# The last down product and the final norm in runs of three, two and one token tiles instead of two runs of three

## The chip, the core and the metric

One NeuronCore of one Trainium2 chip runs the whole program. The metric is the device time of one execution in microseconds (us). The kernel before takes 2925.16 us, the median of three runs (2922.57 to 2926.08).

## What is computed

A two-layer encoder over 256 prompt tokens and 1024 sample tokens, 1024 channels, all in 32-bit floats. Layer 0 mixes with grouped-query attention, layer 1 with a Conformer convolution module; each is followed by a SwiGLU feed-forward network (FFN) of width 2816, and the trunk ends in an RMS norm:

```python
for i in range(DEPTH):
    x = x + mixer(_rms_norm(x, ...))
    x = x + _swiglu(_rms_norm(x, ffn_norm_g[i]), w_gate[i], w_up[i], w_down[i])
return _rms_norm(x, final_norm_g)
```

Here `_swiglu(h) = (silu(h @ w_gate) * (h @ w_up)) @ w_down`, and the norm divides each token's 1024 channels by the root of their mean square and multiplies by `final_norm_g`.

## The kernel before, in words

Activations lie transposed in SBUF: eight tiles `xs[ct]` of 128 channels by tokens. To keep the precision of 32-bit floats each matrix product is made of three matmuls: the left and the right operand are split into a high and a low part (`hl`, `hh`), and high by high, high by low and low by high are added up in PSUM. The tokens go through the layers in two halves; in layer 1 these are CA (tokens 0 to 623) and CB (tokens 624 to 1279, 656 of them). The program's last call is `close(1, rest, xb, CB)`, behind the FFN of CB.

By then all FFN blocks of CB but the last pair of 128 have been multiplied with `w_down` and added to `xs`. `rest` holds that pair. `close` does three things. It multiplies the pair with its rows of `w_down` (`pd`, L1194 to L1197: per channel tile `ct` six matmuls, 2 blocks by 3 parts, of as many columns as the run has tokens). It adds the result to `xs[ct]` (L1200, on VectorE). And it ends with the final norm, for one tile of about 110 tokens at a time: `turn` (L1160) brings the tile to rows of tokens by eight transposes on TensorE into the PSUM tile `fo` (L1164), squares it on ScalarE in two pieces of 512 channels with a sum along the row (L1167, sums in `ssh`), and hands the rest to `finish`, a generator. `finish` adds the two sums (L1172), computes the inverse root on VectorE by a shift and three Newton steps (`rsqrt_steps` and `newton`, L109 to L130: thirteen more operations on one column each), multiplies `fo` by it and by the gain in two pieces (`yo`, L1177), and stores each piece with a DMA from the SyncE queue (L1178).

The tokens are taken in two runs of 328, and each run is three tiles (108, 110, 110). While run 2's channel tiles are multiplied, the tiles of run 1 are turned, one behind each odd `ct`, and `advance(8)` (L1181) takes eight steps of the running generators behind every add from `ct` 3 on, in turns. Behind the last add, `advance(1000)` ends what is still running; then the three tiles of run 2 are turned and finished, with nothing left to multiply.

Two things set the order. `close` stands in a block with `manual_schedule(engines=PE_DVE)` (L1295): TensorE and VectorE execute exactly in the order in which the code issues, so an instruction that waits holds up all behind it on its engine. ScalarE and the queues take what a scheduler gives them. And PSUM is one pool, `pp`, of four buffers of two banks (L640); both `pd` and `fo` come from it (`acc`). A `pd` buffer is free again when its add has read it; a `fo` buffer only when both of its `yo` have.

Of the kernel before, what the change touches and what calls it, by code (L numbers as in the profile page):

```python
# [71 lines left out]
def trunk(ctx: ExitStack, tc: tile.TileContext, a: dict):  # L72
# [33 lines left out]
    def rsqrt_steps(v, shape, scale, eps):  # L106
        rows = shape[0]
        w = small.tile([P, 8], F32, name="rs_w")[:rows, :shape[1]]
        V.tensor_scalar(out=w, in0=v, scalar1=scale, scalar2=eps, op0=ALU.mult, op1=ALU.add)  # L109
        r = small.tile([P, 8], F32, name="rs_r", bufs=5)[:rows, :shape[1]]  # L110
        yield r
        for _ in newton(w, r, *(small.tile([P, 8], dt, name=f"rs_{n}")[:rows, :shape[1]]
                                for n, dt in (("i", I32), ("y", I32), ("t", F32)))):
            yield r
        return r
# [26 lines left out]
    def weights(src, g=None, room=None):  # L142

        raw = wp.tile([P, D], F32, tag="raw", bufs=RAW, name="raw")
        nk = src.shape[1]
        nc.sync.dma_start(raw.rearrange("p (k c) -> p k c", k=nk), src)
        pool, tag, bufs = room or (wp, "hl", WEIGHTS)
        hl = pool.tile([P, 2, D], F32R, tag=tag, bufs=bufs, name="hl")
        if g is None:
            split(hl[:, 0, :], hl[:, 1, :], raw)  # L150
        for k in range(nk if g is not None else 0):
            c = slice(k * D // nk, (k + 1) * D // nk)
            split_scaled(hl[:, 0, c], hl[:, 1, c], raw[:, c], g[:, k:k + 1])
        return hl
# [197 lines left out]
    tiles = [(u, n) for u in us for n in range(len(u.tiles))]  # L352
# [57 lines left out]
    with tc.tile_pool(name="qa", bufs=1) as qa, tc.tile_pool(name="qm", bufs=4, space=PSUM) as qm, \  # L410
# [124 lines left out]
        half = NT // 2  # L535
# [59 lines left out]
        for n, (b, cg) in enumerate(seq):  # L595
            for i in range(half):
                t = b * half + i
# [45 lines left out]
    def slot(name, dt=F32):  # L643
        return sp.tile([P, SLOT], dt, tag="s", name=name)
# [4 lines left out]
    def acc(name):  # L649
        return pp.tile([P, 2, 512], F32, tag="acc", name=name)  # L650
# [502 lines left out]
    def close(layer, rest, xs, half):  # L1153


        n = half.n
        cs = (slice(0, 512), slice(512, D))
        wd = [weights(a["w_down"][layer, f * P:(f + 1) * P, :].unsqueeze(1)) for f, _ in rest]

        def turn(lo, hi):  # L1160
            w = hi - lo
            ps = acc("fo").rearrange("p c n -> p (c n)")[:w]
            for ct in range(NK):
                PE.transpose(ps[:, ct * P:(ct + 1) * P], xs[ct][:, lo:hi], ident)  # L1164
            ss = small.tile([P, 8], F32, name="ssh")
            for k, cc in enumerate(cs):
                S.activation(out=slot("sq")[:w, :512], in_=ps[:, cc], func=AF.Square, accum_out=ss[:w, k:k + 1])  # L1167
            return finish(ps, ss, lo, hi)

        def finish(ps, ss, lo, hi):  # L1170
            w = hi - lo
            V.tensor_tensor(out=ss[:w, 0:1], in0=ss[:w, 0:1], in1=ss[:w, 1:2], op=ALU.add)  # L1172
            yield
            r = yield from rsqrt_steps(ss[:w, 0:1], (w, 1), 1.0 / D, RMS_EPS)
            for cc in cs:
                y = slot("yo")[:w, :512]
                V.scalar_tensor_tensor(out=y, in0=ps[:, cc], scalar=r, in1=gf[:w, cc], op0=ALU.mult, op1=ALU.mult)  # L1177
                nc.sync.dma_start(a["y_sample"][0, half.lo + lo - SP:half.lo + hi - SP, cc], y)  # L1178
                yield

        def advance(steps):  # L1181
            while running and steps:
                g = running.pop(0)
                if next(g, running) is not running:
                    running.append(g)
                steps -= 1

        running, tiles = [], []
        for c in range(2):
            t = slice(c * n, (c + 1) * n)  # L1190
            for ct in range(NK):
                o = slice(ct * P, (ct + 1) * P)
                pd = acc("pd")[:, 0, :n]
                for k, (_, (h, l)) in enumerate(rest):  # L1194
                    for p, x in ((0, h), (0, l), (1, h)):
                        PE.matmul(pd, wd[k][:, p, o], x[:, t], start=k == 0 and p == 0 and x is h,
                                  stop=k == len(rest) - 1 and p == 1)  # L1197
                if ct % 2 == 1 and tiles:
                    running.append(turn(*tiles.pop(0)))
                V.tensor_tensor(out=xs[ct][:, t], in0=pd, in1=xs[ct][:, t], op=ALU.add)  # L1200
                if ct > 2:
                    advance(8)
            cuts = [c * n + n * k // 3 // 2 * 2 for k in range(3)] + [(c + 1) * n]
            tiles = list(zip(cuts, cuts[1:]))
        advance(1000)
        for lo, hi in tiles:
            running.append(turn(lo, hi))
            advance(3)
        advance(1000)
# [85 lines left out]
    with tc.manual_schedule(engines=PE_DVE):  # L1295
        close(1, rest, xb, CB)
# [39 lines left out]
```

## Time and profile before

| | before |
|---|---|
| time, median of 3 runs | 2925.16 us |
| the profiled execution's own time | 2926.48 us |
| its span, first to last instruction | 2924.7 us |
| mean granted TensorE clock | 0.990 |
| TensorE busy | 2837.6 us, 97% |
| VectorE busy | 2291.9 us, 78% |
| ScalarE busy | 1171.2 us, 40% |

The profile shows one execution; its own time is 1.8 us above its span. Busy shares are averages over the whole program. `close` begins at 2887 us from the start of the span and is its last 38 us, so the stretch from there to the end is what has to be read. A granted clock of 1.00 is 2.4 GHz and 0.50 is 1.2 GHz.

### The profile page before, as it was taken

The page shows a single profiled execution, that of the slowest core. Times are in us where ns is not written, and L with a number is a line of the kernel's source. Part 1 is how long each engine was busy: PE and PEld are TensorE (multiplying, and loading weights), DVE is VectorE, ACT ScalarE, POOL GpSimd, SP SyncE. Part 2 cuts the span into 40 slices and gives each one's busy share as a digit, 9 for nine tenths or more (in the row PEclk, how much of TensorE's full clock was granted, in tenths as well). Part 3 has the DMA queues.
Part 4 walks back from the last instruction along what each step waited for, and adds up shares of the span by engine and source line. Part 5 has one row for each costly group of instructions (what it writes and reads, how often), then busy time and mean ns, then how long its engine had stood idle before and what let it go on. Part 6 is the DMA issues. An engine that isn't in the chain of part 4 may idle for free.

```text
span 2924.7 us, 46991 instructions
## 1 busy us (share of the span) xinstructions
PE 2837.6 (97%) x18573; PEld 2717.8 (93%) x18573; DVE 2291.9 (78%) x3741; ACT 1171.2 (40%) x1853; POOL 404.4 (14%) x417
## 2 busy tenths in 40 slices
PE   8998999999999999999999999999999998999997
PEld 6877788789999999999999999999999998999997
DVE  7988999976777777797998666989984538777776
ACT  4538888863433334322111243222223324333332
POOL 2444555420000000010000101110001000000000
PEclk9999999999999999999999999999999999999999
DMA  4513232136777788457676764332324423432221
GB/s 145 189 69 112 51 92 58 45 109 204 257 265 271 274 279 270 126 181 259 217 248 220 277 190 129 115 115 88 99 87 153 128 77 95 134 87 74 86 73 52
DMA packets 316324, 438.68 MB, mean 150 GB/s; under 512 B 22296, under 2 KB 244512, under 8 KB 299208
## 3 DMA queue, kind: packets, MB, share of 16 engines
q1 hardware_dynamic: 298488, 400.10, 42.8%
q0 software_dynamic: 5280, 21.42, 2.0%
q10 hardware_dynamic: 12336, 14.16, 1.4%
q8 instruction: 146, 2.39, 0.3%
q14 instruction: 74, 0.61, 0.1%
HBM read 299.46 MB, written 130.93 MB: 147 GB/s over the span
## 4 chain that ended last, share of the span: by engine, by line
PE 85%; DVE 8%; DMA 3%; issue 2%; ACT 1%; POOL 0%; SPq 0%; DVEq 0%; ACTq 0%; POOLq 0%
PE pd L664 18%; PE ci L1014 8%; PE pg L664 4%; PE pu L664 4%; PE pt L322 4%; PE s L270 4%; PE co L664 4%; PE wo L664 3%; PE z L795 3%; PE z L797 3%; PE z L796 3%; PE v L795 3%; PE v L796 3%; PE v L797 3%; PE y L796 2%; PE y L797 2%
## 5 line engine op out<-in xcount | busy, mean ns | idle before, releaser
L135 ACT CAST hl<-raw 128x1024 fp32r<-128x1024 f32 x328 | 341.2, 1050 | 702.0 <-issue 342.9
L664 PE MATMUL pd<-hh,hl 128*128 128x320 f32 (+2 forms) x2752 | 523.0, 309 | 1.0 <-DVE x L922 0.7
L136 DVE TENSOR_TENSOR hl<-raw,hl 128x1024 fp32r<-128x1024 f32 x328 | 408.3, 1246 | 125.4 <-ACT hl L135 120.0
L1055 DVE SCALAR_TENSOR_TENSOR c<-u,cols,c 128x640 f32<-128x640 f32 (+1 forms) x480 | 429.2, 897 | 8.0
L664 PEld LDWEIGHTS pd<-hh,hl 128*128 128x128 f32 x2752 | 433.4, 188 | 1.8 <-DVE x L922 1.4
L922 DVE TENSOR_TENSOR x<-pd,x 128x640 f32<-128x640 f32 (+2 forms) x304 | 248.6, 823 | 114.8 <-PE pd L664 113.1
L664 PE MATMUL pd<-hl 128*128 128x320 f32 (+2 forms) x1376 | 313.2, 309 | 0.0
L664 PEld LDWEIGHTS pd<-hl 128*128 128x128 f32 x1376 | 230.3, 188 | 0.0
L136 DVE TENSOR_TENSOR pl<-pt,ph 128x512 fp32r<-128x512 f32 x272 | 186.9, 688 | 15.3 <-ACT ph L135 10.8
L282 DVE TENSOR_SCALAR_CACHE_REDUCE s<-s,r_q 128x1024 f32<-128x1024 f32 (+1 forms) x160 | 181.0, 1132 | 20.2 <-PE s L270 13.1
L1014 PE MATMUL ci<-hnh,hl 128*128 128x320 f32 (+2 forms) x1024 | 192.5, 309 | 0.0
L322 PEld LDWEIGHTS pt<-ident,p 128*128 128x128 f32 x1088 | 133.2, 142 | 59.6 <-DVE pl L136 17.2
L315 POOL TENSOR_SCALAR p<-p,rl 128x1024 f32<-128x1024 f32 (+1 forms) x160 | 158.3, 993 | 169.9 <-DVE rl L312 127.1
L135 ACT CAST ph<-pt 128x512 fp32r<-128x512 f32 x272 | 159.7, 589 | 53.7 <-PE pt L322 44.7
L322 PE MATMUL pt<-ident,p 128*128 128x128 f32 x1088 | 167.5, 276 | 13.7 <-DVE pl L136 10.5
L689 POOL TENSOR_TENSOR sq<-sq 128x640 f32<-128x640 f32 (+2 forms) x27 | 51.5, 1906 | 898.9 <-ACT sq L684 555.9
L795 PE MATMUL z<-bh,hl 128*128 128x320 f32 (+1 forms) x528 | 166.1, 315 | 7.9 <-DMA hl<-w_w_up 4.9
L797 PE MATMUL z<-bh,hl 128*128 128x320 f32 (+1 forms) x528 | 165.6, 314 | 2.3 <-DVE hl L136 2.3
L304 ACT ACTIVATE p<-s,nm 128x1024 f32<-128x1024 f32 (+1 forms) x160 | 159.3, 998 | 18.6 <-DVE s L282 18.4
L796 PE MATMUL z<-bl,hl 128*128 128x320 f32 (+1 forms) x528 | 165.5, 313 | 0.0
L1014 PEld LDWEIGHTS ci<-hnh,hl 128*128 128x128 f32 x1024 | 163.9, 188 | 0.0
L664 PE MATMUL pu<-hnh,hl 128*128 128x312 f32 x704 | 132.9, 306 | 0.0
(246 smaller groups left out, 6816.1 us busy)
## 6 DMA issues: line engine op xcount, KB each, us to landing
raw<-in_w_down_dram SPq DMA_DIRECT2D x88, 512.0 KB
raw<-in_w_gate_dram SPq DMA_DIRECT2D x66, 512.0 KB
raw<-in_w_up_dram SPq DMA_DIRECT2D x66, 512.0 KB
w_w_gate<-hl SPq DMA_DIRECT2D x33, 1024.0 KB
w_w_up<-hl SPq DMA_DIRECT2D x33, 1024.0 KB
hl<-w_w_gate SPq DMA_DIRECT2D x33, 1024.0 KB
hl<-w_w_up SPq DMA_DIRECT2D x33, 1024.0 KB
raw<-in_conv_w_in_dram SPq DMA_DIRECT2D x32, 512.0 KB
```

Source lines behind the costliest of these rows:

```text
L135: S.copy(out=dst_h, in_=src)
L136: V.tensor_tensor(out=dst_l, in0=src, in1=dst_h.bitcast(F32), op=ALU.subtract)
L282: V.tensor_scalar(out=s[:, c], in0=s[:, c], scalar1=r_q[self.j // 4][b][:, i, head:head + 1], scalar2=None, op0=ALU.mult, op1=ALU.min, acc ...
L304: S.activation(out=p[:, c], in_=s[:, c], func=AF.Exp, bias=nm[:, i:i + 1], scale=-1.0, accum_out=l[:, i:i + 1])
L322: PE.transpose(ps[:, n * P:(n + 1) * P], self.p[n][:, kt * P:(kt + 1) * P], ident)
L664: PE.matmul(ps[:, c, :n], wt, x[:, c * n:(c + 1) * n], start=first and k == 0 and not end and xi == 0, stop=last and k == nk - 1 and end)
L795: PE.matmul(ps, wh, h, start=first and k == 0, stop=False, skip_group_check=True)
L796: PE.matmul(ps, wh, l, start=False, stop=False, skip_group_check=True)
L797: PE.matmul(ps, wl, h, start=False, stop=k == len(right) - 1, skip_group_check=True)
L922: V.tensor_tensor(out=two(xs[ct], half), in0=pd[:, :, :n], in1=two(xs[ct], half), op=ALU.add)
L1014: PE.matmul(ps[:, c, :hi - lo], wt, x[:, lo:hi], start=k == 0 and not end and xi == 0, stop=k == NK - 1 and end)
L1055: V.scalar_tensor_tensor(out=c[:, :ln], in0=u[:, k:k + ln], scalar=col(ct, R_DW + k), in1=c[:, :ln], op0=ALU.mult, op1=ALU.add)
```

## The change

The six tiles are all laid out at the start (`ends`: 0, 110, 220, 330, 440, 550, 656). The product goes over them in three runs: tiles 1 to 3 (330 tokens), tiles 4 and 5 (220 tokens) and tile 6 (106 tokens). In run 2 the three tiles of run 1 are turned, in run 3 the two of run 2, and behind the last add one tile is left.

```diff
     def close(layer, rest, xs, half):
-        n = half.n
+        step = -(-half.len // 12) * 2
+        ends = [min(k * step, half.len) for k in range(7)]
...
         running, tiles = [], []
-        for c in range(2):
-            t = slice(c * n, (c + 1) * n)
+        for a0, a1 in ((0, 3), (3, 5), (5, 6)):
+            t = slice(ends[a0], ends[a1])
+            n = t.stop - t.start
             for ct in range(NK):
...
                 if ct > 2:
                     advance(8)
-            cuts = [c * n + n * k // 3 // 2 * 2 for k in range(3)] + [(c + 1) * n]
-            tiles = list(zip(cuts, cuts[1:]))
+            tiles = list(zip(ends[a0:a1], ends[a0 + 1:a1 + 1]))
```

Lines behind the new code move down by two or three: the matmuls of `pd` are L1199 in the changed kernel, the transposes L1166, the squares L1169, the sum of the squares L1174, `yo` L1179, its DMA L1180 and the add L1203.

VectorE's order behind the last add, before. `ssh` is the sum of squares, `rs_` are the steps of the inverse root, `yo` the output rows:

```order
L1200 TENSOR_TENSOR x<-pd,x 128x328
L1177 SCALAR_TENSOR_TENSOR yo<-fo,rs_r,gf 110x512
L128 TENSOR_TENSOR rs_t<-rs_t,rs_w 110x1
L1177 SCALAR_TENSOR_TENSOR yo<-fo,rs_r,gf 108x512
L1177 SCALAR_TENSOR_TENSOR yo<-fo,rs_r,gf 110x512
...
L1177 SCALAR_TENSOR_TENSOR yo<-fo,rs_r,gf 110x512 x2
L1172 TENSOR_TENSOR ssh<-ssh 108x1
...
L1177 SCALAR_TENSOR_TENSOR yo<-fo,rs_r,gf 110x512
L130 SCALAR_TENSOR_TENSOR rs_r<-rs_t,rs_r 110x1
L1177 SCALAR_TENSOR_TENSOR yo<-fo,rs_r,gf 110x512 x3
```

Behind the last add stand five of the six `yo` of tiles 1 to 3, then the whole final norm of tiles 4 to 6, their steps taken in turns.

The same place in the changed kernel:

```order
L1203 TENSOR_TENSOR x<-pd,x 128x106
L130 SCALAR_TENSOR_TENSOR rs_r<-rs_t,rs_r 110x1 x2
L1179 SCALAR_TENSOR_TENSOR yo<-fo,rs_r,gf 110x512 x4
L1174 TENSOR_TENSOR ssh<-ssh 106x1
L109 TENSOR_SCALAR rs_w<-ssh 106x1
L119 TENSOR_SCALAR rs_i<-rs_w 106x1
L121 TENSOR_SCALAR rs_y<-rs_i 106x1
L122 TENSOR_SCALAR rs_w<-rs_w 106x1
L126 TENSOR_TENSOR rs_t<-rs_y 106x1
L128 TENSOR_TENSOR rs_t<-rs_t,rs_w 106x1
...
L1179 SCALAR_TENSOR_TENSOR yo<-fo,rs_r,gf 106x512 x2
```

Now the four `yo` of tiles 4 and 5 stand there, and behind them the steps of tile 6 alone.

VectorE's order at the start of run 3, in the changed kernel:

```order
L1179 SCALAR_TENSOR_TENSOR yo<-fo,rs_r,gf 110x512
L1203 TENSOR_TENSOR x<-pd,x 128x220
L1179 SCALAR_TENSOR_TENSOR yo<-fo,rs_r,gf 110x512
L128 TENSOR_TENSOR rs_t<-rs_t,rs_w 110x1
L1179 SCALAR_TENSOR_TENSOR yo<-fo,rs_r,gf 110x512 x2
L130 SCALAR_TENSOR_TENSOR rs_r<-rs_t,rs_y 110x1
L126 TENSOR_TENSOR rs_t<-rs_r 110x1
L1203 TENSOR_TENSOR x<-pd,x 128x106 x4
L128 TENSOR_TENSOR rs_t<-rs_t,rs_w 110x1
L1174 TENSOR_TENSOR ssh<-ssh 110x1 x2
```

Four adds of run 3 follow each other, then the sums of squares of tiles 4 and 5 directly behind one another; the fifth add comes only behind those.

On TensorE the eight transposes of a tile still stand behind every odd channel tile while tiles are left, so those of tiles 4 and 5 stand behind the second and the fourth channel tile of run 3, and those of tile 6 are its last instructions. The product's 96 matmuls of 328 columns have become 48 each of 330, 220 and 106. The weights that a matmul loads are 128 by 128 in all of them, so 48 weight loads are added and the columns stay the same.

## Rows read from the trace of the kernel before

**Rows 1.** The page: the chain that ended last, by engine.
```profile
PE 85%; DVE 8%; DMA 3%; issue 2%; ACT 1%; POOL 0%; SPq 0%; DVEq 0%; ACTq 0%; POOLq 0%
```

**Rows 2.** Busy time by stretch of `close` (length, each engine, clock, DMA share, GB/s).
```profile
2894.00:2907.00 13.00, 11.02 (x75) 9.92 (x73) 7.20 (x45) 3.80 (x12) 0.00 (x0) 1.00 0.01 2
2907.00:2911.00 4.00, 3.01 (x24) 2.55 (x24) 3.76 (x13) 2.15 (x7) 0.00 (x0) 1.00 0.53 170
2911.00:2915.00 4.00, 0.00 (x0) 0.00 (x0) 3.90 (x37) 1.53 (x6) 0.00 (x0) 0.75 0.55 166
2915.00:2920.00 5.00, 0.00 (x0) 0.00 (x0) 4.63 (x14) 0.00 (x0) 0.00 (x0) 0.50 0.47 145
```

**Rows 3.** The chain that ended last, through `close` (start us, length us, what).
```profile
2887.15 9.05 PE pd L1196 x60
2896.20 0.87 PE fo L1164 x8
...
2899.80 1.27 ACT sq L1167 x4
...
2901.09 0.16 DVE ssh L1172
...
2905.26 0.41 DVE x L1200
...
2906.94 0.50 DVE x L1200
```

**Rows 4.** The same chain behind the last add.
```profile
2908.16 1.32 DVE yo L1177 x2
...
2909.78 0.17 DVE rs_t L128
2909.97 0.17 DVE rs_r L130
...
2914.58 0.07 DVE rs_t L128
...
2918.97 0.66 DVE yo L1177
```

**Rows 5.** TensorE in order of time: narrow matmuls elsewhere, and what follows them.
```profile
232.16 0.29 PE L241 MATMUL trq<-ident_r,q 128*128 128x128 f32 x2
232.28 0.47 PE L270 MATMUL s<-k_h,qs 128*128 128x512 f32 x1
...
2416.59 1.91 PE L712 MATMUL bc<-ident,rs_r 82*128 82x82 f32 x16
2418.30 0.53 PE L664 MATMUL pd<-hh,hl 128*128 128x312 f32 x2
```

**Rows 6.** Groups by shape: TensorE's matmuls and weight loads, VectorE's adds (busy, mean ns).
```profile
L1067 PE MATMUL mu<-tot,mean_m 128*128 128x328 f32 x4 | 1.3, 439 | 0.0
L1196 PE MATMUL pd<-hl 128*128 128x328 f32 x32 | 10.1, 314 | 0.0
...
L712 PEld LDWEIGHTS bc<-ident,rs_r 82*128 82x128 f32 x32 | 3.8, 190 | 0.0
L1196 PEld LDWEIGHTS pd<-hl 128*128 128x128 f32 x32 | 6.0, 188 | 0.0
...
L922 DVE TENSOR_TENSOR x<-pd,x 128x656 f32<-128x656 f32 x80 | 67.1, 839 | 48.1 <-PE pd L664 48.1
L1200 DVE TENSOR_TENSOR x<-pd,x 128x328 f32<-128x328 f32 x16 | 8.0, 498 | 5.5 <-PE pd L1196 5.4
```

**Rows 7.** Busy time by stretch at the very end: DMA share and GB/s stand last.
```profile
2916.00:2917.00 1.00, 0.00 (x0) 0.00 (x0) 1.00 (x7) 0.00 (x0) 0.00 (x0) 0.50 0.47 141
...
2922.00:2923.00 1.00, 0.00 (x0) 0.00 (x0) 0.00 (x0) 0.00 (x0) 0.00 (x0) 0.50 0.46 168
```

**Rows 8.** Busy time by stretch earlier, where the granted clock fell.
```profile
2449.00:2452.00 3.00, 0.42 (x1) 0.19 (x1) 3.00 (x6) 2.03 (x3) 3.00 (x1) 1.00 0.00 0
2452.00:2456.00 4.00, 1.46 (x4) 1.05 (x4) 4.00 (x7) 1.94 (x3) 0.67 (x1) 0.53 0.26 92
```

## The prediction

> **What bounds the kernel now.** I read the chain first. TensorE holds 85% of it, VectorE 8% [rows 1]: for nearly the whole program the product is the bound, and nothing there is touched. The change lies in the last 38 us, so I read the busy time by stretch there next. From 2894 to 2907 us TensorE is busy 11.02 of 13 us; then it makes its last transposes, and from 2911 on it does nothing, while VectorE is busy 3.76 of 4, 3.90 of 4 and 4.63 of 5 us [rows 2]. So the end has two parts: up to the last add, TensorE and VectorE in turn; behind it, VectorE alone. The chain says which instruction holds which. Run 1 is matmuls back to back, 60 in 9.05 us, 0.151 us each; eight transposes take 0.87 us [rows 3]. Then the squares of a tile on ScalarE (1.27 us for both pieces), the sum of squares on VectorE that waits for them, and the adds behind it stand on the chain [rows 3]. The last add starts at 2906.94, the last `yo` at 2918.97, which makes 12.03 us of VectorE [rows 3, 4]. From there to the end of the span, 2924.70, it is 5.73 us: the `yo` itself, its DMA, and the wait for the landing.
>
> The idea to be tested is thus that 12 us of VectorE behind the last add become less, because only one tile is left there. The price is what run 3 costs ahead of it.
>
> **The unit prices.** An inverse-root step that needs the one before it starts 0.19 us behind it; with other tiles' steps in between, one follows the other every 0.07 us [rows 4]. A `yo` takes 0.66 us (two in 1.32) [rows 4]. An add of 328 columns holds VectorE 0.41 us [rows 3]; from 328 to 656 columns the duration grows from 498 to 839 ns, 1.04 ns a column [rows 6], so 0.30 us for 220 columns and 0.18 us for 106.
>
> The matmul of 106 or 220 columns is not in the trace. At 0.151 us for 328 columns, the columns alone would give 0.049 and 0.101 us: the lower bound. But each matmul loads its own 128 by 128 weights. The matmuls of 82 columns with a load of 128 columns start 16 times in 1.71 us (2416.59 to 2418.30), 0.107 us each [rows 5], and their load takes 190 ns where ours takes 188 [rows 6]. Against it speak two transposes with 128 columns that take 0.12 us together (232.16 to 232.28) [rows 5]. Upper bound: the 328-column matmul of `mu`, in plain 32-bit floats, takes 439 ns instead of 314 [rows 6], 125 ns more on 151, so nearly two times a column; at that 220 columns cost 0.20 us and 106 cost 0.107. I take 0.107 us for both, since weight load and shape are nearest to `bc`.
>
> The Trainium skill, "TensorE: Matmul & The Clock Gate", section on LDWEIGHTS, puts a load at its columns divided by 1.2 GHz; 128 columns would be 107 ns, and the row of `bc` agrees. The same page's section on the back-to-back issue gap has about 81 ns for a matmul of 128 columns in a stream of load and matmul; by that the sum below would come out 0.4 us lower.
>
> **The change, stretch by stretch.** The order on TensorE and VectorE is fixed, so I walk it with these prices; the same walk over the old order puts its last `yo` at 2918.7 where the trace has 2918.97, 0.3 us off.
>
> Run 1: 48 matmuls with two columns more, 0.04 us. Ends as before.
>
> Run 2, eight channel tiles of 220 columns: 12 matmuls, eight transposes, 12 matmuls, eight transposes before VectorE is first held up by the squares of the second tile. That is 0.5 us less per 12 matmuls; the sum of squares that starts at 2901.09 now [rows 3] would start at 2900.2, and the adds behind it are 0.11 us shorter each. Last add of run 2 at 2905.6, 1.3 us before the old last add.
>
> Run 3 is new, and its eight channel tiles take 2.3 us in columns but about 11 us in the walk. (a) 2.6 us: three of the `yo` of tiles 1 to 3 and a few steps stand ahead of its first add. (b) 2.4 us: four adds; the third and fourth wait for TensorE. Three of the four PSUM buffers are held by `fo`, so the second channel tile starts only when tile 1's second `yo` has freed one, and the transposes of tile 4 and two more channel tiles follow (0.64 and 0.87 us pieces). (c) 2.0 us: the sums of squares of tiles 4 and 5 stand directly behind these adds. Tile 5 is transposed at 2910.2 to 2911.1, its squares end 1.4 us later, and VectorE waits. (d) 4.1 us: the other four adds with two `yo` (1.3 us) and the steps of tiles 3, 4 and 5 in between. The last add comes at 2916.7: 9.7 us later than before.
>
> Behind it: two steps, four `yo` of tiles 4 and 5 (2.6 us), then the thirteen dependent steps of tile 6 with nothing left to put between them (thirteen times 0.19, 2.5 us), and its first `yo`. The squares of tile 6 are hidden behind the four `yo`. That puts the last `yo` at 2922.8, 6.1 us behind the last add instead of 12.0: 5.9 us gained. What was moved off the end has come back as run 3, because tiles 4 and 5 cannot be finished before tiles 1 to 3 let go of PSUM and of VectorE.
>
> The stores: before, the last six leave at the pace of the `yo`. The DMA engines take them up half-way through 2916 to 2917 and end them half-way through 2922 to 2923 [rows 7], from about 2916.2 to 2922.6: 6.4 us for six, 1.07 us each, so the last one queues. Now four leave at 2917.8 to 2919.8 and are through by 2922.7, and the last two go out at 2922.9 and 2923.6 and end at 2925.6. That is 3.0 us later than 2922.6, so 1.0 us less than the shift of the `yo`, 3.8 (2922.8 less 2919.0).
>
> Sum: 9.7 later, less 5.9, less 1.0: **2.8 us slower**. The profiled execution took 2926.48 us; with 2.8 us that is 2929.3. It stands 1.3 us above the median of the runs, 2925.16, so the median should go to **2928.0 us**, 0.1% up. A measurement of this kernel can tell about 0.2%, 5.9 us, from no change, so this is no change.
>
> **The bounds.** At 0.049 and 0.101 us a matmul, the same walk ends 0.6 us earlier (2.2 us slower than before): TensorE is not what run 3 waits for. At the upper bound it ends 2.7 us later (5.5 us slower).
>
> **Rivals.** (1) The narrow matmul is dearer than its columns and its load, at more than twice a column. No product in the trace has these operands with so few columns, so nothing excludes it. From 2.1 times a column the end would be over 5.9 us later; at four times the walk gives 18 us for the `yo`, 17 in the sum: 2942. For it: `mu`'s nearly doubled duration; against it: `bc` and the short transposes.
>
> (2) TensorE's clock falls in run 3. Before, the clock stays at 1.00, 2.4 GHz, while TensorE is busy 11.02 of 13 and 3.01 of 4 us [rows 2]. At 2452 it fell to 0.53 on average, near 1.2 GHz, after 3 us in which TensorE was busy 0.42 us [rows 8]. In the walk it is busy 1.7 of the 4 us from 2911 to 2915, in between. If matmuls and transposes take double from 2914 on, the last `yo` is 1.2 us later still; from 2911 on 1.8 us; from 2909.6 on 3.2 us: 2929 to 2931. The same page of the Trainium skill, in its section on the clock's oscillation, warns of just this, bursts of matmuls with waits between them, and the rows at 2449 to 2456 agree.
>
> (3) Some of the waits (b) and (c) are shorter than walked, since ScalarE's and TensorE's part overlaps more. Both gone would give back about 3.5 us, so 2924.5. To be faster by 0.2% takes more: VectorE's own work from 2894 on is about 19.5 us (7.20, 3.76, 3.90 and 4.63) [rows 2] plus 0.5 us for eight more adds; even with no wait at all it ends at 2914, 5.6 us before the old end of the last `yo`. The idea that one tile at the end instead of three saves what two tiles cost there, some 6 us, needs that bound to be met.
>
> **How the numbers follow.** The forecast, 2926 to 2930: 0.6. Rival 1: 0.12, over the 0.2% bound (2931.0) for most of it. Rival 2: 0.16, over the bound in a third of it. Rival 3: 0.12, 2921.5 to 2926. Slower by over 0.2%: 0.11 and 0.05, and 0.02 for the runs' own spread: 0.18. Faster: 0.03, for what the walk may have missed in rival 3. The range goes from rival 3's better half, 2923.5, to the clock's worst case with a little spread, 2932: it leaves out most of rival 1 and a corner of rival 3.
>
> **What would show it.** Right: the last add about 10 us later than 2906.9; a wait of VectorE of about 2 us at a sum of squares in run 3, for ScalarE; thirteen steps 0.19 us apart ahead of the last two `yo`; a store queue that is empty before the last two. Matmuls of 106 columns 0.107 us apart. Wrong: a last add before 2914, or one after 2918; matmuls of 106 or 220 columns over 0.2 us apart; or a clock below 1.00 before the last transposes.

## The result, and the profile after

The change makes the kernel slower: 2941.84 us, the median of four runs (2939.93 to 2942.74), beside 2925.62 us before on the same chip (2922.57 to 2928.0). The ratio is 1.0054, with a 95% interval of 1.0042 to 1.0065: 16.2 us, where 2.8 were forecast, and outside the range. Three executions in the runs below took over half a millisecond longer than the others of their kernel and are left out of all medians and ratios. The profiled execution of the changed kernel took 2939.93 us; its span is 2938.2 us.

Two executions reach `close` a few us apart (run 1's first matmul starts at 2886.99 before and at 2884.91 after), so the end is compared by distances inside it: from run 1's first matmul to the start of the last add, from there to the start of the last `yo`, from there to the end of the span (which is read to 0.1 us).

| us | to last add | to last `yo` | to the end | sum |
|---|---|---|---|---|
| before | 19.95 | 12.03 | 5.73 | 37.7 |
| after | 34.77 | 6.41 | 12.11 | 53.3 |
| difference | +14.8 | -5.6 | +6.4 | +15.6 |
| predicted | +9.7 | -5.9 | -1.0 | +2.8 |

The middle column came as forecast. The other two did not, and they make up the 12.8 us between forecast and profile: 5.1 ahead of the last add, 7.4 behind the last `yo`.

The stretches of the new end, in the columns of [rows 2]:

```profile
2897.00:2900.00 3.00, 1.86 (x17) 1.68 (x17) 1.89 (x19) 1.08 (x4) 0.00 (x0) 1.00 0.00 0
2900.00:2904.00 4.00, 2.12 (x16) 1.58 (x14) 2.67 (x21) 1.27 (x4) 0.00 (x0) 1.00 0.01 2
2904.00:2907.00 3.00, 2.74 (x14) 2.61 (x15) 2.38 (x8) 0.00 (x0) 0.00 (x0) 0.56 0.54 156
2907.00:2915.00 8.00, 7.05 (x35) 6.89 (x33) 1.69 (x15) 2.53 (x8) 0.00 (x0) 0.50 0.15 54
2915.00:2925.00 10.00, 6.01 (x26) 5.40 (x26) 8.51 (x46) 1.27 (x4) 0.00 (x0) 0.50 0.38 116
...
2926.00:2927.00 1.00, 0.00 (x0) 0.00 (x0) 0.75 (x2) 0.00 (x0) 0.00 (x0) 0.50 0.04 10
2927.00:2937.00 10.00, 0.00 (x0) 0.00 (x0) 0.00 (x0) 0.00 (x0) 0.00 (x0) 0.50 0.13 43
```

Two things stand out. The granted clock goes from 1.00 to 0.50, that is to 1.2 GHz, early in the stretch from 2904 on and stays there; from 2907 to 2915 TensorE is busy 7.05 of 8 us and VectorE 1.69, so TensorE sets the pace there, at half its clock. And the 10 us from 2927 on hold nothing but DMA, at a share of 0.13 and 43 GB/s; before, the stores' stretches that are shown had shares of 0.46 and more, and 141 GB/s and more [rows 2, 7].

TensorE in order of time (start, length, instruction; in brackets how long it stood idle and for whom) shows where the clock fell:

```profile
2899.24 1.09 PE L1166 MATMUL fo<-ident,x 128*110 128x128 f32 x8 [1.14 <-DVE x L1203]
...
2900.80 0.27 PE L1199 MATMUL pd<-hl 128*128 128x220 f32 x1
2900.91 0.28 PE L1199 MATMUL pd<-hh,hl 128*128 128x220 f32 x1
2902.51 0.37 PE L1199 MATMUL pd<-hh,hl 128*128 128x220 f32 x1 [1.33 <-DVE rs_i L119]
...
2903.99 0.32 PE L1199 MATMUL pd<-hh,hl 128*128 128x106 f32 x1 [0.56 <-DVE x L1203]
2904.14 0.27 PE L1199 MATMUL pd<-hl 128*128 128x106 f32 x1
2904.26 0.53 PE L1199 MATMUL pd<-hh,hl 128*128 128x106 f32 x2
...
2905.47 0.42 PE L1199 MATMUL pd<-hh,hl 128*128 128x106 f32 x1 [0.26 <-DVE yo L1179]
2905.69 0.41 PE L1199 MATMUL pd<-hl 128*128 128x106 f32 x1
```

Two matmuls of 220 columns start 0.11 us apart, and the first three of 106 columns 0.15 and 0.12; then they take 0.41 instead of 0.27 and come 0.22 apart. In front stand three waits of TensorE on VectorE of 1.14, 1.33 and 0.56 us, all in run 2 or at its end.

The chain of waits through run 3 and behind it (the rows of before are [rows 3, 4]):

```profile
2903.64 0.29 DVE x L1203
...
2905.47 1.49 PE pd L1199 x6
2906.96 1.73 PE fo L1166 x8
...
2912.95 1.27 ACT sq L1169 x4
...
2914.24 0.16 DVE ssh L1174
...
2916.84 2.81 PE pd L1199 x12
...
2919.68 0.27 DVE x L1203
2919.95 0.14 DVE rs_r L130 x2
2920.08 2.69 DVE yo L1179 x4
...
2924.68 0.17 DVE rs_t L126
...
2924.87 0.17 DVE rs_t L128
...
2925.34 0.75 DVE yo L1179
2926.09 0.66 DVEq L1334
```

Eight transposes take 1.73 us instead of 0.87 [rows 3], and twelve narrow matmuls stand directly ahead of the last add with 2.81 us. Behind it lie the four `yo`, the steps 0.19 us apart and the two `yo` of tile 6, as the prediction drew it (the second one is the piece from 2926.09 on, which the chain books to VectorE's queue).

The DMA of the end in 40 slices (about 1.2 us each: busy share in tenths, then GB/s), with its packets:

```profile
DMA  0000000000035660000003440476401111111000
GB/s 0 0 0 13 0 0 0 0 7 0 0 69 180 223 228 21 0 0 0 0 0 69 157 134 0 128 257 182 154 13 29 34 44 52 51 51 52 20 0 0
DMA packets 1428, 2.71 MB, mean 54 GB/s; under 512 B 114, under 2 KB 114, under 8 KB 1426
```

The same line of packets for the kernel before:

```profile
DMA packets 1450, 2.71 MB, mean 54 GB/s; under 512 B 136, under 2 KB 136, under 8 KB 1448
```

The bytes are the same; the last two stores, 424 KB, go out at about 51 GB/s. The number of small packets is the key: 136 before and 114 after. Before there are 8 stores of 110 rows and 4 of 108; after 10 of 110 and 2 of 106. The largest divisors up to 16 are 11, 12 and 2, and 8 x 11 + 4 x 12 = 136, 10 x 11 + 2 x 2 = 114: one small packet for each DMA engine that a store uses. So 106 rows (2 x 53) go over two engines of sixteen, which is a share of 2/16, the 0.13 in the row. The Trainium skill, "DMA: Bandwidth & Descriptors", section "Why a DMA increments its semaphore by 16 and not by 1", states this rule: the largest number up to 16 that divides the slowest dimension of both sides. The trace agrees in every count of this case.

### The profile page after: what moved, and what is told of

The parts are those of the page before. It is cut to its first block, busy times and chain, and to the rows that moved or that the text cites. A ratio compares the mean times of both kernels' runs of the same rounds, so it can differ in the third digit from the quotient of the medians.

```text
span 2938.2 us, 47094 instructions
## 1 busy us (share of the span) xinstructions
PE 2848.5 (97%) x18621; PEld 2729.9 (93%) x18621; DVE 2292.9 (78%) x3749; ACT 1172.0 (40%) x1853; POOL 404.4 (14%) x417
## 4 chain that ended last, share of the span: by engine, by line
PE 85%; DVE 8%; DMA 2%; issue 2%; ACT 1%; POOL 0%; SPq 0%; DVEq 0%; ACTq 0%; POOLq 0%
PE pd L664 18%; PE ci L1014 8%; PE pg L664 4%; PE pu L664 4%; PE pt L322 4%; PE s L270 4%; PE co L664 4%; PE wo L664 3%; PE z L795 3%; PE z L797 3%; PE z L796 3%; PE v L795 3%; PE v L796 3%; PE v L797 3%; PE y L796 3%; PE y L797 3%
## 5 line engine op out<-in xcount | busy, mean ns | idle before, releaser
L282 DVE TENSOR_SCALAR_CACHE_REDUCE s<-s,r_q 128x1024 f32<-128x1024 f32 (+1 forms) x160 | 181.0, 1132 | 19.6 <-PE s L270 12.8
L135 ACT CAST ph<-pt 128x512 fp32r<-128x512 f32 x272 | 159.7, 590 | 52.7 <-PE pt L322 44.1
L304 ACT ACTIVATE p<-s,nm 128x1024 f32<-128x1024 f32 (+1 forms) x160 | 159.4, 999 | 18.7 <-DVE s L282 18.4
```

Of the source, the lines that this page charges most:

```text
L135: S.copy(out=dst_h, in_=src)
L282: V.tensor_scalar(out=s[:, c], in0=s[:, c], scalar1=r_q[self.j // 4][b][:, i, head:head + 1], scalar2=None, op0=ALU.mult, op1=ALU.min, acc ...
L304: S.activation(out=p[:, c], in_=s[:, c], func=AF.Exp, bias=nm[:, i:i + 1], scale=-1.0, accum_out=l[:, i:i + 1])
```

## The experiments

Two theories, each for one of the two gaps. **Stores:** the tile of 106 rows leaves through two DMA engines, and that costs what stands behind the last `yo`. **Clock:** TensorE's clock falls ahead of run 3, and that costs what the last add comes later than walked. The rivals were that narrow matmuls are dear by themselves (the prediction's first rival), and that the three runs cost all of it whatever the tiles. Medians are compared with the kernel before on the same chip. Distances of all profiles, as in the table above; "fell" is the granted clock's first fall to 0.50, counted from run 1's first matmul. Where it falls ahead of the last add it stays down up to it, but for e3_wide and e9_wide_again, where it is back at 1.00 from 22.6 to 29.4 us.

| us | to last add | to last `yo` | to the end | sum | fell |
|---|---|---|---|---|---|
| before | 19.95 | 12.03 | 5.73 | 37.7 | 26.0 |
| after | 34.77 | 6.41 | 12.11 | 53.3 | 19.4 |
| e1_rows16 | 34.83 | 6.36 | 4.08 | 45.3 | 19.1 |
| e2_two_106 | 19.95 | 12.01 | 13.91 | 45.9 | 26.2 |
| e5_two_rows16 | 19.96 | 12.00 | 4.18 | 36.1 | 28.8 |
| e6_two_102 | 19.91 | 12.01 | 6.91 | 38.8 | 26.4 |
| e7_106_first | 19.94 | 12.03 | 8.69 | 40.7 | 26.6 |
| e3_wide | 31.99 | 6.33 | 12.02 | 50.3 | 19.2 |
| e9_wide_again | 32.01 | 6.34 | 12.09 | 50.4 | 19.2 |
| e4_rows16_wide | 30.94 | 6.28 | 4.03 | 41.3 | 28.8 |
| e8_change_again | 34.78 | 6.42 | 12.05 | 53.3 | 18.7 |
| e10_fill | 33.69 | 6.33 | 4.08 | 44.1 | 30.1 |
| e11_rows16_again | 34.03 | 6.36 | 4.12 | 44.5 | 21.6 |

### The stores

**e1_rows16**: three runs as in the change, with tiles of 112 tokens and a last one of 96.

```diff
-        step = -(-half.len // 12) * 2
+        step = 112
```

> Runs of three, two and one tiles as in the change, but the tiles are 112, 112, 112, 112, 112 and 96 tokens instead of 110 five times and 106. Theory (stores): the last two stores of the change, of 106 rows, run on 2 of the 16 DMA engines (DMA share 0.12 to 0.14 from 2927 to 2937 us); 96 rows divide over 16, so the end comes about 4.5 us behind the last yo instead of 12.2, and the time is 7 to 8 us under the change's: about 2934 us, 8 us over before. Rival (the end is slow for another reason, the last stores being alone or TensorE's clock being down): within 2 us of the change, 2940 to 2943 us.

Measured: 2934.40 us, 1.0026 [1.0014, 1.0037] of before, so +7.6 where the change has +16.2. The part behind the last `yo` falls from 12.11 to 4.08, the rest stays. Its DMA from 2894 on:

```profile
DMA  0000000000000057870000000016600489502820
GB/s 0 0 0 0 16 0 0 0 0 0 8 0 0 0 164 236 254 256 8 0 0 0 0 0 0 0 31 199 199 31 0 129 277 303 203 6 72 246 76 0
DMA packets 1506, 2.71 MB, mean 68 GB/s; under 512 B 192, under 2 KB 192, under 8 KB 1504
```

192 small packets are 12 x 16, and the last two stores pass in one short burst. Stores hold: 8 us.

**e2_two_106**: the change's tiles alone, in two runs as before.

```diff
-        for a0, a1 in ((0, 3), (3, 5), (5, 6)):
+        for a0, a1 in ((0, 3), (3, 6)):
```

> The change's tiles (110 five times, 106 last) in two runs of three tiles, as before. Theory (stores): the last add and the last yo stay where they were before, within 0.3 us, and the two stores of 106 rows alone put the end 6 to 7 us later: about 2932 us. Rival (the long end belongs to the third run): as before, 2924 to 2927 us.

Measured: 2934.64 us, 1.0026 [1.0016, 1.0036], +7.9. Up to the last `yo` it is the kernel before to 0.02 us; then it takes 13.91 us instead of 5.73, a little more than the 6 to 7 us expected. So the tiles alone make the kernel 8 us slower; three runs are not needed for it. The end of it by stretch:

```profile
2917.00:2920.00 3.00, 0.00 (x0) 0.00 (x0) 0.04 (x1) 0.00 (x0) 0.00 (x0) 0.50 0.38 112
2920.00:2925.00 5.00, 0.00 (x0) 0.00 (x0) 0.00 (x0) 0.00 (x0) 0.00 (x0) 0.50 0.13 44
2925.00:2930.00 5.00, 0.00 (x0) 0.00 (x0) 0.00 (x0) 0.00 (x0) 0.00 (x0) 0.50 0.10 40
```

**e5_two_rows16**: both of these edits, two runs and tiles of 112 with a last one of 96.

```diff
-        step = -(-half.len // 12) * 2
+        step = 112
...
-        for a0, a1 in ((0, 3), (3, 5), (5, 6)):
+        for a0, a1 in ((0, 3), (3, 6)):
```

> Two runs of three tiles, as before, with tiles of 112 five times and 96 tokens instead of 108, 110, 110, 108, 110, 110. Theory (stores): every store now divides over 16 DMA engines instead of 12 or 11, so the last six queue less: last add and last yo as before, the end about 4.2 us behind the last yo instead of 5.8, 1.5 us under before: 2925 us where before is 2926.5, at the edge of what can be told. Rival (11 engines were enough): as before.

Measured: 2923.69 us (2921.97 to 2926.64) beside 2924.22, 0.9996 [0.9987, 1.0005]. In the profile the part behind the last `yo` is 4.18 instead of 5.73, the 1.5 us expected; the runs don't tell it from before. It is the best kernel of this study, and no proven gain.

**e6_two_102** (two runs as in e2_two_106; the dose between: 102 rows in the last tile, divisor 6):

```diff
-        ends = [min(k * step, half.len) for k in range(7)]
+        ends = [0, 112, 222, 332, 442, 554, 656]
```

> Two runs of three tiles, the last tile of 102 tokens (112, 110, 110, 110, 112, 102). Theory (a store runs on the largest number of DMA engines up to 16 that divides its rows): 102 rows run on 6 engines, at about 0.38 of the 16, so the two last stores take about 3 us instead of the 9.5 of 106 rows, and the end comes 6 to 7 us behind the last yo: 2927 to 2928 us, 1 us over before. Rival (rows of a tile that is shorter than the others are slow in themselves): about as with 106 rows, 2933 us.

Measured: 2926.25 us, 1.0006 [0.9997, 1.0015]. Its packets:

```profile
DMA packets 1456, 2.71 MB, mean 68 GB/s; under 512 B 142, under 2 KB 142, under 8 KB 1454
```

Tiles of 112, 110, 110, 110, 112 and 102 rows, two stores each, make 64 + 66 + 12 = 142. With 2, 6 and 16 engines for the last tile, the part behind the last `yo` is 13.91, 6.91 and 4.18 us. The dose goes the right way (about as the theory said, and far from the rival's 2933), and 102 rows would hardly have been noticed by the time alone.

**e7_106_first** (two runs as in e2_two_106; the tile of 106 rows comes first, not last):

```diff
-        ends = [min(k * step, half.len) for k in range(7)]
+        ends = [0] + [half.len - k * step for k in range(5, -1, -1)]
```

> Two runs of three tiles, the tile of 106 tokens first instead of last. Theory (stores): its two stores still run on 2 engines for about 9 us, but 11 us before the end, beside VectorE's work for the other tiles, so the end is as before within 1 us, 2926 to 2928 us. Rival (any store of 106 rows costs its 7 us wherever it stands, because later stores queue behind it): 2933 us.

Measured: 2927.90 us, 1.0014 [1.0004, 1.0023], +3.7: a miss, for it was to be as before within 1 us, and the rival's 2933 did not come either. The 106 rows were issued first and still 8.69 us pass behind the last `yo`, 3.0 more than before. Its end by stretch:

```profile
2920.00:2922.00 2.00, 0.00 (x0) 0.00 (x0) 0.00 (x0) 0.00 (x0) 0.00 (x0) 0.50 0.70 241
2922.00:2924.00 2.00, 0.00 (x0) 0.00 (x0) 0.00 (x0) 0.00 (x0) 0.00 (x0) 0.50 0.34 128
2924.00:2926.00 2.00, 0.00 (x0) 0.00 (x0) 0.00 (x0) 0.00 (x0) 0.00 (x0) 0.50 0.13 51
```

From 2924 on the share is again 0.13, two engines, though the last store has 110 rows and eleven engines: two of them are late. So a bad tile costs even when it isn't the last. That the two late engines are those of the first tile, and that the stores behind queue there, is inferred from the share and not shown.

### The clock

**e3_wide**: the change, but a run of fewer than 256 columns multiplies 256; the columns ahead of its own are multiplied again and not read.

```diff
+            w = max(n, 256)
+            tw = slice(t.stop - w, t.stop)
...
-                pd = acc("pd")[:, 0, :n]
+                pd = acc("pd")[:, 0, :w]
...
-                        PE.matmul(pd, wd[k][:, p, o], x[:, t], start=k == 0 and p == 0 and x is h,
+                        PE.matmul(pd, wd[k][:, p, o], x[:, tw], start=k == 0 and p == 0 and x is h,
...
-                V.tensor_tensor(out=xs[ct][:, t], in0=pd, in1=xs[ct][:, t], op=ALU.add)
+                V.tensor_tensor(out=xs[ct][:, t], in0=pd[:, w - n:], in1=xs[ct][:, t], op=ALU.add)
```

> The change, but the matmuls of runs 2 and 3 take 256 columns (the run's own and those in front of it; the add reads the run's own alone), so TensorE streams 256 columns where it streamed 220 and 106. Theory (clock): at 2.4 GHz a matmul of 106 columns costs about as much as one of 256, because its weight load sets the pace (0.107 against 0.117 us), and the busier array keeps the clock at 1.00 through run 3: the last yo comes about 4.5 us earlier than the change's, 2937 us in all. Rival (the clock falls for the waits, not for the narrow matmuls): it falls at the same place, the last yo is 1 to 2 us later than the change's, 2943 us.

Measured: 2943.54 us (2935.78 to 2944.02), 1.0053 [1.0038, 1.0068]. By its time it is inconclusive: it is as slow as the change on another chip. Its profiled execution reached `close` 7 us later than the change's, and took 50.3 us there instead of 53.3. So it was repeated beside the change.

**e8_change_again** and **e9_wide_again**: the change and e3_wide once more, on one chip.

> The change as it is, on the same chip as the next kernel, for comparison. Expected as measured: 15 to 16 us over before.

> The change with the matmuls of runs 2 and 3 at 256 columns, as in the earlier run, whose four times were 2935.8 and three near 2943.7. Theory (clock, with its phase): the wider stream makes the clock fall later or for a shorter time, so that most runs are 3 to 5 us under the change; the median 2938 to 2940 us, with a spread of some 8 us. Rival (the columns do not matter, the waits alone do): the same median as the change, within 1 us.

Measured: 2942.00 us, 1.0050 [1.0036, 1.0064], and 2938.49 us, 1.0040 [1.0027, 1.0052]. The medians are 3.5 us apart, but the two intervals overlap; in the profiles the wide kernel is 2.8 us earlier at the last add (34.78 and 32.01), with more than twice the columns in run 3. So the columns are not what run 3 waits for. The clock of e9_wide_again falls as early as the change's, and comes back:

```profile
2905.00:2908.00 3.00, 2.84 (x13) 2.82 (x14) 2.55 (x8) 0.00 (x0) 0.00 (x0) 0.50 0.50 145
2909.00:2915.00 6.00, 4.23 (x35) 3.82 (x33) 2.75 (x24) 2.54 (x8) 0.00 (x0) 1.00 0.11 41
2915.50:2918.50 3.00, 3.00 (x16) 2.99 (x16) 2.25 (x18) 0.00 (x0) 0.00 (x0) 0.50 0.51 149
```

Up to the last add it stands at 0.50 for 6.0 us here, and for 16.1 in e8_change_again. The runs timed without a profile go the same way: the mean granted clock of the whole execution is 0.983 to 0.986 in the five runs of the change and 0.987 to 0.989 in the five of the wide one.

**e4_rows16_wide**: the edits of e1_rows16 and of e3_wide together.

```diff
-        step = -(-half.len // 12) * 2
+        step = 112
...
+            w = max(n, 256)
+            tw = slice(t.stop - w, t.stop)
...
```

> Both edits: tiles of 112 five times and 96, and matmuls of 256 columns in runs 2 and 3. If both theories hold, what is left of the change is the walk of the prediction: last yo 4 to 5 us later than before, end 4 to 4.5 us behind it: 2928 to 2930 us, 3 to 4 us over before. If only the stores matter, 2935 us; if only the clock, 2937 us.

Measured: 2929.72 us, the median of nine runs, +2.9, with a ratio of 1.0019 [1.0009, 1.0028], which is 2.6 to 8.2 us; in the profile, +3.6 (41.3 and 37.7). Beside e1_rows16 on the same chip the median is 4.7 less, the profile 4.0. TensorE at its run 3, and then its stretches:

```profile
2905.39 0.39 PE L1201 MATMUL pd<-hh,hl 128*128 128x256 f32 x1 [0.52 <-DVE x L1205]
2905.61 0.28 PE L1201 MATMUL pd<-hl 128*128 128x256 f32 x1
2905.73 0.40 PE L1201 MATMUL pd<-hh,hl 128*128 128x256 f32 x2
```

```profile
2909.00:2914.00 5.00, 3.58 (x29) 3.16 (x27) 2.37 (x21) 2.18 (x8) 0.00 (x0) 1.00 0.07 25
2914.00:2918.00 4.00, 3.61 (x18) 3.56 (x19) 3.45 (x22) 0.00 (x0) 0.00 (x0) 0.61 0.37 115
```

At full clock 256 columns come 0.12 us apart behind the first one, and the clock holds to 2914.9. The same widening had not held it in e9_wide_again, so 256 columns alone don't decide it. Within the nine runs of this one kernel time and clock go together: the six with a mean granted clock of 0.989 or 0.990 took 2928.89 to 2931.72 us, the three with 0.986 to 0.988 took 2932.80 to 2936.43. This kernel is near the prediction's walk without its two faults: 11.0 us more to the last add where 9.7 were walked, and +3.6 in all in the profile where the walk had +2.8.

**e10_fill** and **e11_rows16_again**: e1_rows16 with one matmul of 512 columns per channel tile of runs 2 and 3, into the half of the PSUM buffer that nobody reads, and e1_rows16 again beside it.

```diff
-                pd = acc("pd")[:, 0, :n]
+                banks = acc("pd")
+                pd = banks[:, 0, :n]
...
+                if a0 > 0:
+                    PE.matmul(banks[:, 1, :], wd[0][:, 0, o], rest[0][1][0][:, :512], start=True, stop=True)
```

> Tiles of 112 five times and 96 in runs of three, two and one, narrow matmuls as in the change, and one matmul more for each channel tile of runs 2 and 3: 512 columns into the bank of the pd buffer that nothing reads (16 in all, about 0.23 us each at 2.4 GHz). Theory (clock): TensorE waits in run 3 anyway; the added work fills the waits, keeps the clock at 1.00, and the narrow matmuls go at 0.107 us again. By the walk the added work costs 1.9 us, the clock gives back 5 us: about 3 us under the same kernel without it, 6 us over before. Rival (the clock is not what run 3 pays for): the added work costs its 2 to 4 us, 10 to 12 us over before.

> The same kernel without the added matmuls, on the same chip, for comparison: 7 to 8.5 us over before, the clock at 0.50 for nearly all of run 3.

Measured: 2936.59 us, 1.0038 [1.0024, 1.0052], and 2933.23 us, 1.0026 [1.0016, 1.0035]. A miss: the filled kernel is not 3 us faster; its median is 3.4 us higher, though the intervals overlap. Its profile shows the clock held through most of run 3:

```profile
2906.00:2909.00 3.00, 2.30 (x17) 1.68 (x15) 2.90 (x8) 0.00 (x0) 0.00 (x0) 1.00 0.46 141
2909.00:2916.00 7.00, 5.82 (x47) 5.22 (x45) 2.83 (x24) 2.53 (x8) 0.00 (x0) 1.00 0.21 71
2916.00:2921.00 5.00, 4.65 (x20) 4.07 (x20) 3.33 (x22) 0.00 (x0) 0.00 (x0) 0.57 0.32 95
```

and a matmul of 96 columns every 0.11 us there. Then the clock falls after all, and each added matmul holds TensorE for over half a us, the last one directly ahead of the last add at 2920.29:

```profile
2919.69 0.57 PE pd L1203
```

In the one profiled execution the two effects cancel (44.1 us in `close`, 44.5 and 45.3 without). The clock was up in the other runs too: the mean granted clock of the whole execution is 0.988 to 0.989 in the five runs with the filling and 0.985 to 0.988 in the nine without. So the filling did to the clock what was expected, and no time was won by it.

## Why the prediction was wrong, step by step

**The stores (predicted -1.0, measured +6.4): failed.** The step "the last two go out at 2922.9 and 2923.6 and end at 2925.6" priced a store of 106 rows like one of 110, from the pace of six stores in [rows 7]. (By its own numbers the term is also 0.8 and not 1.0 us, 3.8 less 3.0, and the sum 3.0 instead of 2.8; this changes nothing.) The pace depends on the number of rows: two engines instead of eleven. Everything about the start was right: the queue is empty before the last two (a share of 0.04 around 2926.5), and they start when their `yo` are done. e1_rows16 takes this term back and e2_two_106 shows it alone, 8 us each. The diff's tile ends were walked for their width in tokens only, and the output side of a tile, rows over DMA engines, was never priced: this is the omission, and no rival had it.

**Run 3 (predicted +9.7, measured +14.8): the mechanism right, the clock wrong.** The second rival, "TensorE's clock falls in run 3", was the right thing at the wrong place. The prediction looked for idle time in run 3, and put the fall at 2909.6 at the earliest, for 3.2 us; counted from the same first matmul it came at 2906.4. The waits that went ahead of the fall are those of run 2: its matmuls start 0.11 us apart instead of 0.151, VectorE's work between them became little shorter, so TensorE was busy 1.86 of 3 and 2.12 of 4 us, and the clock was down 0.4 us into run 3. The step "TensorE is not what run 3 waits for" rested on prices at full clock: the 48 matmuls and sixteen transposes of run 3 are 6.9 us at 0.107 and 0.109 us each, twice that at half clock, and 5.1 us were measured on top of the walk. The pair e1_rows16 and e4_rows16_wide gives 3.9 us to the last add back with the clock up longer, the pair of the change and e9_wide_again 2.8. In e4 the clock still fell 2.1 us ahead of the last add, so some of the remaining 1.3 us to the walk may be clock as well. That stays open, and so does what decides the moment: in [rows 2] 3.01 busy of 4 left the clock up, and the same e1 kernel fell once at 19.1 and once at 21.6 us. The Trainium skill, "TensorE: Matmul & The Clock Gate", section on the clock's oscillation, was cited for this rival. The trace agrees with its warning of bursts with waits between them, but not with its case, in which the waits are longer and for DMA: here none of TensorE's in run 2 was over 1.33 us. The rival was given 0.16 where it came to pass, and far too small a price.

**Narrow matmuls (0.107 us taken): right at full clock.** There a matmul starts 0.11 us behind the one before it for 220 columns, 0.12 to 0.15 for the first three of 106, 0.11 for 96 (e10_fill), 0.12 for 256. The first rival named 2942, and 2941.84 came; but its mechanism, a narrow matmul at more than twice its columns, is refuted by these rows: at half clock they come 0.21 to 0.22 us apart, 106 columns in the change as 256 in e9_wide_again, and more columns end earlier (e9 against e8). The number met by coincidence: 7 to 8 us of stores and some 5 us of run 3, most of it clock, are in it.

**Run 2 and the pieces of run 3.** Run 2 was right: its last add, the add at 2903.64 in the chain, starts 18.7 us behind run 1's first matmul, 1.2 us ahead of the old last add (1.3 walked). Piece (a), three `yo` and some steps, takes 2.5 us to run 3's first add at 2906.16 (2.6 walked): VectorE alone, and right. The rest in VectorE's order of time (run 3's first four adds, then the sum of squares):

```profile
2906.16 0.26 DVE L1203 TENSOR_TENSOR x<-pd,x 128x106 f32<-128x106 f32 x1
2907.00 0.27 DVE L1203 TENSOR_TENSOR x<-pd,x 128x106 f32<-128x106 f32 x1 [0.58 <-PE pd L1199]
2909.88 0.27 DVE L1203 TENSOR_TENSOR x<-pd,x 128x106 f32<-128x106 f32 x1 [2.62 <-PE pd L1199]
2911.16 0.27 DVE L1203 TENSOR_TENSOR x<-pd,x 128x106 f32<-128x106 f32 x1 [1.01 <-PE pd L1199]
...
2914.24 0.16 DVE L1174 TENSOR_TENSOR ssh<-ssh 110x1 f32<-110x1 f32 x1 [2.68 <-ACT sq L1169]
```

Piece (b), four adds with TensorE's transposes and channel tiles between them, takes 5.4 us up to the wait for the squares, where 2.4 were walked; (c), that wait, 2.7 instead of 2.0, since the transposes ahead of the squares are slow too; (d), from there to the last add at 2919.68, 5.4 instead of 4.1. Together 4.9 us more, which is the 5.1 of the term but for 0.2, and it lies in the pieces in which VectorE waits for TensorE. The third rival, shorter waits, fell: they grew. Of the signs of being wrong that the prediction named, a last add after 2918 (2921.8, counted from the same first matmul), matmuls over 0.2 us apart and a clock below 1.00 before the last transposes came.

**Behind the last add (predicted 5.9 less, measured 5.6): right**, with the steps that need one another 0.19 us apart and four `yo` in 2.69 us.

**The sum without the two faults** was near: e4_rows16_wide, with no store through two engines and the clock up for most of run 3, is at +3.6 in its profile (+2.9 by the medians) where +2.8 were summed. So the idea of the change, one tile behind the last add instead of three, fails for the reason forecast (run 3 costs more ahead of the last add than it saves behind it), and the larger part of the 16.2 us is made of two things that the walk held constant.

## What to carry to other kernels

Where a change sets new tile sizes, factor the rows of every store: the trace of before shows how many engines a store uses (small packets per store, DMA share at the end), and 106 rows in the last tile cost 8 us beside 110. Where matmuls are made shorter between waits that stay, look at the clock in that stretch too, and not only in the new one behind it: here the clock was down 0.4 us into the new stretch, and TensorE's matmuls and transposes there came at half their pace. A walk of the instruction order is only as good as the prices that it takes as fixed.

## What the runs showed that was not expected

- A store here used as many DMA engines as the largest divisor up to 16 of its rows (112, 110, 108, 106, 102 and 96 rows): 136, 114, 192 and 142 small packets for four sets of tiles, each count met exactly, and 51 GB/s for two engines.
- A store on few engines costs even when others follow it: 106 rows in the first of six tiles still cost 3.0 us behind the last `yo` (8.69 instead of 5.73).
- At full clock a matmul with its own load of 128 by 128 weights came every 0.11 to 0.12 us from 96 to 256 columns, behind the first ones of a group; so the columns saved by a narrower run, below 256, saved almost nothing on TensorE.
- More useless work can end earlier: 256 columns instead of 106 ended the product 2.8 us (e9 against e8) and 3.9 us earlier (e4 against e1), with the clock up for longer. A separate filling matmul gave the clock back and no time (e10).
